# Gate rows formed inside the last projection block, and the gate tiles shared out anew between attention, sample and the loads for the last products

## The chip, the core and the metric

One NeuronCore of a Trainium2 chip runs the whole program. The metric is the time of one execution on the device in microseconds (us). TensorE (PE in the profile, with PEld for its weight loads) does the matmuls, VectorE (DVE), ScalarE (ACT) and GpSimd (POOL) the rest. Every transfer of this kernel is issued by the sync engine's queue (SP, SPq), which works through its list in order: an issue that waits for its data or its buffer holds up all issues behind it. Each engine likewise takes its own list in order.

## The reference

One layer of a hybrid decoder trunk for 1024 prompt rows and 32 sample rows (8 sequences of 4 new tokens). With fp32 inputs:

```
h = rmsnorm(x)
pool_in, pool_z, qk_pre, v, o_pre, m_z, if_pre, gate_pre = split(h @ w_in)
a  = (multiscale_pool(pool_in) * silu(pool_z)) @ w_pool_down
q, k = split(silu(causal_conv(qk_pre)))
i, f = split(if_pre + b_if)                 # 4 heads each: the gate rows
hc = mlstm_chunkwise(q, k, v, i, f, state)  # chunks of 128 rows, running C, n, m
bm = (head_rmsnorm(hc * sigmoid(o_pre)) * silu(m_z)) @ w_mlstm_down
g_a, g_b = split(sigmoid(gate_pre))         # 2 x 1024 columns: the gate tiles
x = x + (g_a * a + g_b * bm) @ w_out
x = x + (pe @ w_ple) * sigmoid(rmsnorm(x) @ w_ple_gate);  y = rmsnorm(x)
```

The sample rows use the same formulas with a state `C` of 512x512 per sequence and head (32 of them, 1 MB each), which is read, updated and written back.

## The kernel before

Every fp32 product is made from high and low parts: a tile is split into `whi` (ACT, line 286 or 288) and `wlo` (DVE, line 292 or 294), and `mm3` (lines 299 to 301) issues three matmuls for each 128 rows of the contraction. `load_w` (line 320) brings 256 columns of a weight in two halves through two buffers `wraw`.

The stages stand one behind the other in `run`:

1. `norm_in` and 20 projection blocks (q, k, v, o, z for each of 4 heads; `half_product`, line 603), which write q, k, v, o, z to DRAM. Near the end `plain_h` rebuilds the normalised input `hh`, `hl`.
2. `gates` forms the 8 gate rows i and f (48 matmuls of 352 columns, line 652), sends them through DRAM (`g8D`) and makes the decay tables of all chunks (`dt`, lines 767 and 790).
3. `merge_gates(range(8))`: 8 groups of 256 gate columns. A group is 6 chunks of 24 matmuls of 352 columns (three chunks are here called one gate tile: 128 columns for all 1056 rows; a group has two), each chunk evicted by a sigmoid (`sz`, line 1192) and each tile stored to DRAM (`sgD`, line 1194).
4. `attn`: 16 pairs of chunks (4 heads x 4). A pair loads `qk`, `v`, `o`, `zz` (lines 826 and 873; `v`, `o`, `zz` have one buffer each), makes two `num` products, updates `C` (the `kv` products) and transposes the result `o` (`attn_turn`, line 948). The buffer of `num` is single, so the second `num` of a pair waits until DVE has formed `o` from the first (line 936), which needs the loaded `o`.
5. `sample`: 32 steps; each loads a state `ct` (line 1051), multiplies it (`num`, line 1053), updates it (`kv`, line 1057; DVE line 1058) and stores it (line 1061), with three buffers. It ends with `hcS`, the sample rows of `hc`.
6. `pool_branch`: 4 groups, each 12 chunks of 24 matmuls against `hh`, `hl` and 6 short chunks against `poh`, `pol`.
7. `hc_tiles` loads the attention's result into `mvhA`, `mvlA` (buffers named `sz` again), then `downs` and two closing stages make the last products.

Stages overlap by a generator: `feed` sets work aside in the background, and each `fm` over the full contraction ends with `tick`, which takes `rate` further steps of it. Gates and attention are fed to the gate tiles, the sample to `pool_branch`. A scheduler then puts the instructions of all engines in a fixed order, so program order is a priority and not the final order.

Of the kernel before, what the change touches and what calls it, by code (L numbers as in the profile page):

```python
# [11 lines left out]
F32R = mybir.dt.float32r  # L12
AF = mybir.ActivationFunctionType
ALU = mybir.AluOpType
# [4 lines left out]
P = 128  # L19
# [4 lines left out]
NT = T + NS  # L24
H, DH = 4, 512
M = H * DH
KT = D // P
L = 128
NCH = T // L
CW = NT // 3  # L30
# [13 lines left out]
O_GB = O_GA + D  # L44


RATE_A, RATE_S = 10.0, 2.1
HT = T // 2


# [210 lines left out]
class Trunk:  # L261
# [369 lines left out]
                                      rhs=raw[k // 4][f][:, k % 4, :], start=k < 4, stop=k >= 4)  # L631
        return ps

    def gates(self):


        nc, I, O = self.nc, self.I, self.O
        a, d, c = self.ap_, self.dp, self.cp2
        raw = self.t(a, [P, KT, 8], "gw")
        nc.sync.dma_start(raw, I["w_in"][:, O_IF:O_IF + 8].rearrange("(k p) n -> p k n", p=P))  # L640
        wg = self.t(a, [P, KT, P], "gwh", F32R)
        nc.gpsimd.memset(wg.bitcast(F32), 0.0)
        self.hi(wg[:, :, 0:8], raw)
        self.lo(wg[:, :, 32:40], raw, wg[:, :, 0:8])
        g8 = self.t(a, [8, NT], "g8")
        g8l = self.t(a, [8, NT], "g8l")
        for j in range(3):
            s = slice(j * CW, (j + 1) * CW)
            ps = self.mmps()
            for k in range(KT):  # L650
                for x in range(2):
                    nc.tensor.matmul(ps[:, :CW], lhsT=wg[:, k], rhs=self.hmov[k][x][:, s], start=k == 0 and x == 0,
                                     stop=k == KT - 1 and x == 1)
            nc.scalar.activation(g8l[:, s], ps[32:40, :CW], AF.Copy)
            nc.vector.tensor_tensor(out=g8[:, s], in0=ps[0:8, :CW], in1=g8l[:, s], op=ALU.add)
        gD = self.t(d, [8, NT], "g8D")
        nc.sync.dma_start(gD, g8)
        yield True
        R, W = H * NCH, L + DS
        gi = self.t(a, [R, W], "gi")  # L660
        gf = self.t(a, [R, W], "gf")
# [31 lines left out]
        ps = self.miscps()  # L693
# [7 lines left out]
        for h in range(H):  # L701
# [11 lines left out]
                                op=ALU.subtract)  # L713
        nc.vector.tensor_tensor(out=half(rows[:, 2], 0), in0=half(rows[:, 2], 1), in1=half(en[:, 0], 0), op=ALU.add)
        ps = self.miscps()
# [12 lines left out]
        g = self.t(a, [R, W], "gg")  # L728
# [25 lines left out]
        ps = self.miscps()  # L754
# [8 lines left out]
        for h in range(H):  # L763
# [5 lines left out]
            for j in range(NCH // 2):  # L769
                for x in (0, 2):  # L770
                    nc.vector.scalar_tensor_tensor(out=dt[:, j, x], in0=dt[:, j, x], scalar=col(0, 2 * j + x // 2),
                                                   in1=self.cmask, op0=ALU.add, op1=ALU.add)
# [647 lines left out]
    def run(self):  # L1420
# [9 lines left out]
        d = self.dp  # L1430
# [29 lines left out]
        for n, _ in enumerate(blocks):  # L1460
            if n == 20 * 7 - 2 - 4:
                self.plain_h()
        _g.close()
        _w.close()
        _x.close()
# [8 lines left out]
        _m.close()  # L1474
        self.ap_, _a = self.pool("gates", "right")
        gates = self.gates()
        next(gates)
        self.pp, _p = self.pool("gates2")
        _s = []

        def rest():
            self.rate = 1.6
            yield from gates
            _a.close()
            self.atp, _at = self.pool("attn", "right")
            self.attn_setup()
            self.rate = RATE_A
            yield from self.attn()
            _at.close()
            self.sp, st = self.pool("sample", "right")  # L1490
            _s.append(st)
            self.rate = RATE_S
            yield from self.sample()
        self.feed(rest(), 1.6)
        self.merge_gates(range(8))
        while not _s:
            next(self.bg)
        _p.close()
# [2 lines left out]
        _p.close()  # L1501
        self.mpA, _ma = self.pool("movA")
        self.pp, _p = self.pool("gates3")
        first = self.hc_tiles(self.pp, 0, "A", "sz")
        self.drain()
        _s[0].close()
        _p.close()
# [39 lines left out]
```

## Time and profile before

| what | value |
|---|---|
| median of 3 runs | 2294.91 us (2289.3 to 2297.19) |
| the profiled execution | 2293.93 us, its span 2292.2 us |
| TensorE busy | 2191.0 us, 96% of the span |
| VectorE, ScalarE, GpSimd busy | 1247.5, 898.6, 139.9 us |
| mean granted TensorE clock | 0.976 of 2.4 GHz |
| the chain that ended last | PE 89%, DMA 6%, DVE 2% |
| moved to and from HBM | 310 MB, 135 GB/s over the span |

The table is read against TensorE: the rest of the span, some 101 us, is time in which it ran no matmul, and at a granted clock of 0.5 (1.2 GHz) its work takes twice as long.

### The profile page before, as it was taken

The page shows a single profiled execution, that of the slowest core. Times are in us where ns is not written, and L with a number is a line of the kernel's source. Part 1 is how long each engine was busy: PE and PEld are TensorE (multiplying, and loading weights), DVE is VectorE, ACT ScalarE, POOL GpSimd, SP SyncE. Part 2 cuts the span into 40 slices and gives each one's busy share as a digit, 9 for nine tenths or more (in the row PEclk, how much of TensorE's full clock was granted, in tenths as well). Part 3 has the DMA queues.
Part 4 walks back from the last instruction along what each step waited for, and adds up shares of the span by engine and source line. Part 5 has one row for each costly group of instructions (what it writes and reads, how often), then busy time and mean ns, then how long its engine had stood idle before and what let it go on. Part 6 is the DMA issues. An engine that isn't in the chain of part 4 may idle for free.

```text
span 2292.2 us, 37165 instructions
## 1 busy us (share of the span) xinstructions
PE 2191.0 (96%) x15071; PEld 1993.7 (87%) x15071; DVE 1247.5 (54%) x2063; ACT 898.6 (39%) x1634; POOL 139.9 (6%) x319
## 2 busy tenths in 40 slices
PE   5999999999999999899999999999994999999998
PEld 4789888989898989899999998877772999999998
DVE  7846465646644665336565665655664334443545
ACT  5535444534454454444333343322231431223443
POOL 2101010001100110000000000000000000000000
PEclk7999999999999999999999999999995999999999
DMA  4333332333232331384656454667766524323112
GB/s 140 98 99 104 98 106 74 112 101 108 74 120 88 100 103 53 107 282 135 202 169 198 152 168 161 204 246 271 262 217 217 166 94 131 104 75 132 52 47 81
DMA packets 235836, 312.52 MB, mean 136 GB/s; under 512 B 13722, under 2 KB 168946, under 8 KB 235664
## 3 DMA queue, kind: packets, MB, share of 16 engines
q1 hardware_dynamic: 235664, 310.15, 41.5%
q8 instruction: 118, 1.93, 0.3%
q14 instruction: 54, 0.44, 0.1%
HBM read 200.01 MB, written 110.45 MB: 135 GB/s over the span
## 4 chain that ended last, share of the span: by engine, by line
PE 89%; DMA 6%; DVE 2%; ACT 1%; issue 1%; SPq 0%; POOL 0%; DVEq 0%; POOLq 0%; ACTq 0%
PE mm L603 35%; PE mm L299 12%; PE mm L301 12%; PE mm L300 12%; PE misc L630 2%; PE num L1053 2%; PE misc L838 2%; DMA ct<-state_mlstm_C 2%; PE num L299 2%; PE num L300 1%; PE num L301 1%; PE kv L299 1%; DMA new_C_sample<-ct 1%; PE kv L300 1%; PE kv L301 1%; PE kv L1057 1%
## 5 line engine op out<-in xcount | busy, mean ns | idle before, releaser
L292 DVE TENSOR_TENSOR wlo<-wraw,whi 128x1024 fp32r<-128x1024 f32 (+1 forms) x196 | 235.2, 1200 | 275.9 <-ACT whi L286 273.5
L286 ACT ACTIVATE whi<-wraw 128x1024 fp32r<-128x1024 f32 (+1 forms) x196 | 203.6, 1039 | 241.9 <-PE mm L603 94.6
L299 PE MATMUL mm<-hh,whi 128*128 128x352 f32 x768 | 252.1, 328 | 6.3 <-ACT sz L1192 5.3
L301 PE MATMUL mm<-hh,wlo 128*128 128x352 f32 x768 | 251.8, 328 | 0.0
L300 PE MATMUL mm<-hl,whi 128*128 128x352 f32 x768 | 250.8, 327 | 0.0
L603 PE MATMUL mm<-whi,hl 128*128 128x256 f32 x768 | 217.6, 284 | 0.0
L603 PE MATMUL mm<-wlo,hh 128*128 128x256 f32 x768 | 214.8, 280 | 0.0
L603 PE MATMUL mm<-whi,hh 128*128 128x256 f32 x768 | 214.7, 281 | 0.0
L299 PEld LDWEIGHTS mm<-hh,whi 128*128 128x128 f32 x768 | 145.7, 190 | 12.2 <-ACT sz L1192 5.6
L242 DVE SCALAR_TENSOR_TENSOR z<-z,vcols,z 128x512 f32<-128x512 f32 (+1 forms) x192 | 143.9, 774 | 21.7 <-ACT z L240 14.6
L301 PEld LDWEIGHTS mm<-hh,wlo 128*128 128x128 f32 x768 | 145.8, 190 | 10.1 <-issue 9.2
L300 PEld LDWEIGHTS mm<-hl,whi 128*128 128x128 f32 x768 | 146.2, 190 | 7.5 <-issue 6.7
L603 PEld LDWEIGHTS mm<-whi,hh 128*128 128x128 f32 x768 | 145.0, 189 | 5.7 <-ACT part L256 3.3
L1058 DVE SCALAR_TENSOR_TENSOR ct<-ct,dec,kv 128x512 f32<-128x512 f32 x128 | 92.2, 742 | 98.1 <-PE kv L1057 75.7
L603 PEld LDWEIGHTS mm<-wlo,hh 128*128 128x128 f32 x768 | 144.5, 188 | 0.4
L603 PEld LDWEIGHTS mm<-whi,hl 128*128 128x128 f32 x768 | 144.4, 188 | 0.4
L97 ACT ACTIVATE s<-mm 128x512 f32<-128x512 f32 x120 | 71.4, 595 | 147.4 <-PE mm L603 146.0
L301 PE MATMUL mm<-mvhB,wlo 128*128 128x352 f32 x384 | 123.0, 321 | 0.8 <-DVE wlo L294 0.8
L300 PE MATMUL mm<-mvlB,whi 128*128 128x352 f32 x384 | 122.8, 321 | 0.0
L299 PE MATMUL mm<-mvhB,whi 128*128 128x352 f32 x384 | 119.7, 323 | 0.0
L603 PE MATMUL mm<-hh,whi 128*128 128x512 f32 x256 | 102.7, 402 | 1.4 <-DVE n4l L498 1.3
L603 PE MATMUL mm<-hl,whi 128*128 128x512 f32 x256 | 102.4, 400 | 1.3 <-DVE hl L292 1.3
(435 smaller groups left out, 5794.9 us busy)
## 6 DMA issues: line engine op xcount, KB each, us to landing
wraw<-w_in SPq DMA_DIRECT2D x112, 512.0 KB
ct<-state_mlstm_C SPq DMA_DIRECT2D x32, 1024.0 KB
new_C_sample<-ct SPq DMA_DIRECT2D x32, 1024.0 KB
qkD<-z SPq DMA_DIRECT2D x64, 256.0 KB
qk<-qkD SPq DMA_DIRECT2D x16, 1024.0 KB
sgD<-sz SPq DMA_DIRECT2D x16, 528.0 KB
sg<-sgD SPq DMA_DIRECT2D x16, 528.0 KB
vD<-z SPq DMA_DIRECT2D x32, 256.0 KB
```

What stands on the lines that cost most here:

```text
L97: tr.nc.scalar.activation(s, x, AF.Copy)
L242: nc.vector.scalar_tensor_tensor(out=acc[:, :tot], in0=z[:, o:o + tot], scalar=wc(o), in1=acc[:, :tot], op0=ALU.mult, op1=ALU.add)
L286: self.nc.scalar.activation(out, in_, AF.Copy)
L292: self.nc.vector.tensor_tensor(out=out, in0=in_, in1=hi.bitcast(F32), op=ALU.subtract)
L299: mm(ps, lhsT=sh, rhs=mh, start=start, stop=False)
L300: mm(ps, lhsT=sh, rhs=ml, start=False, stop=False)
L301: mm(ps, lhsT=sl, rhs=mh, start=False, stop=stop)
L603: mm(out, lhsT=st[k], rhs=mv[k], start=start and opens and k == 0 and n == 0, stop=stop and k == 3 and n == 2, skip_group_check=True)
L630: self.nc.tensor.matmul(ps[g, f * 256:(f + 1) * 256], lhsT=self.hs[:, k, :], rhs=raw[k // 4][f][:, k % 4, :], start=k < 4, stop=k >= 4)
L838: nc.tensor.matmul(out, lhsT=qk[:, 4 + d, i * L:(i + 1) * L], rhs=qk[:, d, i * L:], start=d == 0, stop=d == 3)
L1053: nc.tensor.matmul(num[32 * d:32 * d + 32, 0, :], lhsT=qm[:, b * P + d * NS:b * P + (d + 1) * NS], rhs=ct[:, d, :], start=b == 0, stop=b = ...
L1058: nc.vector.scalar_tensor_tensor(out=ct[:, d, :], in0=ct[:, d, :], scalar=self.dec[:, h * DB + b, 1:2], in1=kv, op0=ALU.mult, op1=ALU.add)
```

## The change

The gate rows move from the start of `gates` into a function `gate_rows`, called with `plain_h` inside the last projection block; they borrow its buffers (`z`, `whi`) and are stored in three parts. `attn` is taken at 16 steps for a gate tile, not 10, the sample at 1.85, not 2.1. Six groups of gate columns stay beside gates and attention; group 6 now stands behind `pool_branch`, and group 7 behind the loads of `hc_tiles`.

```diff
--- before.py
+++ after.py
@@ -44,7 +44,7 @@
 O_GB = O_GA + D
 
 
-RATE_A, RATE_S = 10.0, 2.1
+RATE_A, RATE_S = 16.0, 1.85
 HT = T // 2
 
 
@@ -631,19 +631,16 @@
                                       rhs=raw[k // 4][f][:, k % 4, :], start=k < 4, stop=k >= 4)
         return ps
 
-    def gates(self):
-
-
-        nc, I, O = self.nc, self.I, self.O
-        a, d, c = self.ap_, self.dp, self.cp2
-        raw = self.t(a, [P, KT, 8], "gw")
+    def gate_rows(self):
+
+        nc, I, g = self.nc, self.I, self.gp
+        raw = self.t(g, [P, 3 + HT + 56], "z", bufs=self.nz)[:, :KT * 8].rearrange("p (k n) -> p k n", k=KT)
         nc.sync.dma_start(raw, I["w_in"][:, O_IF:O_IF + 8].rearrange("(k p) n -> p k n", p=P))
-        wg = self.t(a, [P, KT, P], "gwh", F32R)
+        wg = self.t(self.wp, [P, KT, P], "whi", F32R, bufs=3)
         nc.gpsimd.memset(wg.bitcast(F32), 0.0)
         self.hi(wg[:, :, 0:8], raw)
         self.lo(wg[:, :, 32:40], raw, wg[:, :, 0:8])
-        g8 = self.t(a, [8, NT], "g8")
-        g8l = self.t(a, [8, NT], "g8l")
+        self.g8D = self.t(self.dp, [8, NT], "g8D")
         for j in range(3):
             s = slice(j * CW, (j + 1) * CW)
             ps = self.mmps()
@@ -651,11 +648,17 @@
                 for x in range(2):
                     nc.tensor.matmul(ps[:, :CW], lhsT=wg[:, k], rhs=self.hmov[k][x][:, s], start=k == 0 and x == 0,
                                      stop=k == KT - 1 and x == 1)
-            nc.scalar.activation(g8l[:, s], ps[32:40, :CW], AF.Copy)
-            nc.vector.tensor_tensor(out=g8[:, s], in0=ps[0:8, :CW], in1=g8l[:, s], op=ALU.add)
-        gD = self.t(d, [8, NT], "g8D")
-        nc.sync.dma_start(gD, g8)
-        yield True
+            g8 = self.t(g, [P, 3 + HT + 56], "z", bufs=self.nz)[:8, :CW]
+            nc.scalar.activation(g8, ps[32:40, :CW], AF.Copy)
+            nc.vector.tensor_tensor(out=g8, in0=ps[0:8, :CW], in1=g8, op=ALU.add)
+            nc.sync.dma_start(self.g8D[:, s], g8)
+
+    def gates(self):
+
+
+        nc, I, O = self.nc, self.I, self.O
+        a, d, c = self.ap_, self.dp, self.cp2
+        gD = self.g8D
         R, W = H * NCH, L + DS
         gi = self.t(a, [R, W], "gi")
         gf = self.t(a, [R, W], "gf")
@@ -1460,6 +1463,7 @@
         for n, _ in enumerate(blocks):
             if n == 20 * 7 - 2 - 4:
                 self.plain_h()
+                self.gate_rows()
         _g.close()
         _w.close()
         _x.close()
@@ -1474,7 +1478,6 @@
         _m.close()
         self.ap_, _a = self.pool("gates", "right")
         gates = self.gates()
-        next(gates)
         self.pp, _p = self.pool("gates2")
         _s = []
 
@@ -1492,7 +1495,7 @@
             self.rate = RATE_S
             yield from self.sample()
         self.feed(rest(), 1.6)
-        self.merge_gates(range(8))
+        self.merge_gates(range(6))
         while not _s:
             next(self.bg)
         _p.close()
@@ -1501,7 +1504,9 @@
         _p.close()
         self.mpA, _ma = self.pool("movA")
         self.pp, _p = self.pool("gates3")
+        self.merge_gates(range(6, 7))
         first = self.hc_tiles(self.pp, 0, "A", "sz")
+        self.merge_gates(range(7, 8))
         self.drain()
         _s[0].close()
         _p.close()
```

The scheduler's order shows the change at three places. Buffer numbers are part of the names.

First the sync queue around the end of the last block. `z` are the block's results, `zD` their place in DRAM, `wraw` the weights of the first gate columns, `gw` the raw weights of the gate rows. Before:

```order
L177 DMA zD_16_75<-z_8825 128x2x256
L177 DMA zD_16_75<-z_8878 128x2x256
L320 DMA wraw_8998<-w_in 128x4x256
L320 DMA wraw_9004<-w_in 128x4x256
L177 DMA zD_16_75<-z_8882 128x2x256
L640 DMA gw_8928<-w_in 128x8x8
L668 DMA bif_9091<-b_if 32x1x1 x2
```

and now:

```order
L177 DMA zD_16_75<-z_8841 128x2x256
L177 DMA zD_16_75<-z_8948 128x2x256
L320 DMA wraw_9001<-w_in 128x4x256
L320 DMA wraw_9007<-w_in 128x4x256
L177 DMA zD_16_75<-z_8952 128x2x256
L669 DMA gi_9092<-g8D_8717 32x1x128
L670 DMA gi_9092<-g8D_8717 32x1x4
```

The two `wraw` loads stand behind the last but one store of the block in both; the gate rows' weights are gone from here (they are loaded earlier), and reading the rows back (`gi`) now follows the block's last store at once.

Second, TensorE at a change of pairs in the attention, from the last transposes of one pair's `o` towards the second `num` of the next pair. In the kernel before, at the change from the tenth to the eleventh pair:

```order
L948 MATMUL misc_12442<-ident_112,o_12216 128x128 x4
L300 MATMUL num_12548<-Cl_9637,qh_12370 128x256
L301 MATMUL num_12548<-Ch_9636,ql_12371 128x256
L894 MATMUL misc_12594<-ident_112,qk_12355 128x128 x4
L299 MATMUL mm_12931<-hh_135,whi_12459 128x352
L300 MATMUL mm_12931<-hl_136,whi_12459 128x352
L301 MATMUL mm_12931<-hh_135,wlo_12460 128x352
```

and at the same change now:

```order
L951 MATMUL misc_12273<-ident_112,o_11967 128x128 x4
L897 MATMUL misc_12333<-ident_112,qk_12186 128x128 x4
L897 MATMUL misc_12394<-ident_112,qk_12186 128x128 x4
L299 MATMUL kv_12403<-vhi_1233_9628,kh_1698_12338 128x258
L300 MATMUL kv_12403<-vlo_1235_9630,kh_1698_12338 128x258
L299 MATMUL kv_12411<-vhi_1233_9628,kh_1698_12338 128x256
L300 MATMUL kv_12411<-vlo_1235_9630,kh_1698_12338 128x256
L301 MATMUL kv_12403<-vhi_1233_9628,kl_1699_12339 128x258
L299 MATMUL kv_12403<-vhi_1234_9629,kh_1707_12399 128x258
L300 MATMUL kv_12403<-vlo_1236_9631,kh_1707_12399 128x258
L301 MATMUL kv_12411<-vhi_1233_9628,kl_1699_12339 128x256
L299 MATMUL kv_12411<-vhi_1234_9629,kh_1707_12399 128x256
```

Before, 23 gate matmuls (`mm<-hh`, `mm<-hl`) stand among the 65 from these transposes to that second `num`; now it is 28 matmuls in all and none of them a gate's. Of the attention's `num` and `kv` matmuls (1632) 347 stood behind the last gate tile before, and 816 do now: heads 2 and 3 run without gate tiles beside them. Short changes of pair, with under 50 matmuls from the transposes to the second `num`, were two before, the last two with 39 and 37; now there are seven, with 32, 28, 45, 35, 45, 45 and 37, which is 267 together.

Third, TensorE at the end of the sample. Before, its last steps and the last transposes ran straight into the last products (`mm<-mvhA`):

```order
L1057 MATMUL kv_16743<-vst_16200,km_16732 128x512
L1053 MATMUL num_14232<-ct_16734,qm_14233 32x512 x4
L1065 MATMUL num_14232<-voz_16885,sel_120 32x512
L1057 MATMUL kv_16746<-vst_16200,km_16732 128x512
L1057 MATMUL kv_16749<-vst_16200,km_16732 128x512
L1071 MATMUL num_14232<-voz_16888,pb_14149 128x512
L1080 MATMUL misc_16904<-ident_112,shc_16895 128x128 x4
L1174 MATMUL misc_16969<-ident_112,np_2004_14285 47x128 x4
L1174 MATMUL misc_16985<-ident_112,np_2004_14285 47x128 x4
L299 MATMUL mm_17141<-mvhA_17010,whi_17119 128x352
```

Now they lie between the gate tiles of groups 6 and 7:

```order
L300 MATMUL mm_16784<-hl_136,whi_16605 128x352
L301 MATMUL mm_16784<-hh_135,wlo_16606 128x352
L1068 MATMUL num_13891<-voz_16810,sel_120 32x512
L1074 MATMUL num_13891<-voz_16813,pb_13808 128x512
L299 MATMUL mm_16876<-hh_135,whi_16865 128x352
L300 MATMUL mm_16876<-hl_136,whi_16865 128x352
L301 MATMUL mm_16876<-hh_135,wlo_16866 128x352
```

and the last products follow the last gate chunk:

```order
L299 MATMUL mm_17008<-hh_135,whi_16871 128x352
L300 MATMUL mm_17008<-hl_136,whi_16871 128x352
L301 MATMUL mm_17008<-hh_135,wlo_16872 128x352
L299 MATMUL mm_17144<-mvhA_16841,whi_17122 128x352
L300 MATMUL mm_17144<-mvlA_16842,whi_17122 128x352
L301 MATMUL mm_17144<-mvhA_16841,wlo_17123 128x352
```

On VectorE and ScalarE the splits of `mvhA` and `mvlA` moved ahead of the sigmoids of group 7: the first sigmoid of group 7 stands behind the last of the four splits.

## Rows read from the trace of the kernel before

**Rows 1.** Stretches: length, busy time by engine (x instructions), granted clock, DMA share, GB/s.

```profile
922.00:1000.00 78.00, 65.24 (x387) 64.00 (x386) 30.50 (x101) 39.09 (x51) 3.38 (x6) 0.91 0.58 169
1000.00:1360.00 360.00, 359.89 (x2634) 356.00 (x2633) 204.73 (x390) 137.66 (x274) 15.29 (x26) 1.00 0.58 185
1360.00:1420.00 60.00, 54.63 (x436) 52.44 (x435) 40.48 (x90) 23.25 (x48) 4.91 (x9) 0.96 0.35 111
1420.00:1710.00 290.00, 279.19 (x1603) 224.09 (x1603) 164.44 (x301) 75.91 (x138) 13.11 (x37) 0.98 0.69 240
1710.00:1775.00 65.00, 33.23 (x115) 17.39 (x114) 31.44 (x63) 13.03 (x30) 0.89 (x3) 0.65 0.66 232
```

**Rows 2.** The chain that ended last, 905 to 945 us: start, length, what.

```profile
908.76 1.22 DVE hl L292 x2
...
910.71 11.38 PE mm L603 x94
922.09 5.14 DMA wraw<-w_in
927.25 1.07 ACT whi L286
...
929.85 9.87 PE mm L652 x48
939.88 0.16 PE mm L300
```

**Rows 3.** TensorE's waits, 920 to 1000 us: in total, times, longest.

```profile
PE mm L652 <- DVE gwh L292: 7.4, 1, 7.4
PE mm L299 <- ACT sz L1192: 5.3, 1, 5.3
```

**Rows 4.** TensorE's instructions at the last two changes of pair, idle time before in brackets.

```profile
1377.61 0.55 PE L948 MATMUL misc<-ident,o 128*128 128x128 f32 x3 [0.29 <-DVE o L941]
...
1386.92 0.36 PE L299 MATMUL num<-Ch,qh 128*128 128x258 f32 x1 [2.12 <-DVE o L936]
...
1399.38 0.66 PE L948 MATMUL misc<-ident,o 128*128 128x128 f32 x4
...
1405.61 0.36 PE L299 MATMUL num<-Ch,qh 128*128 128x258 f32 x1 [0.69 <-DVE o L936]
```

**Rows 5.** The sync queue's issues of loads at these two changes of pair.

```profile
1376.92 0.37 SPq L873 DMA_DIRECT2D v<-vD  x1
1377.58 0.37 SPq L873 DMA_DIRECT2D zz<-zD  x1
1378.30 0.36 SPq L873 DMA_DIRECT2D o<-oD  x1
...
1400.07 0.36 SPq L873 DMA_DIRECT2D o<-oD  x1
```

**Rows 6.** The chain that ended last, 1355 to 1420 us.

```profile
1378.30 7.63 DMA o<-oD
```

**Rows 7.** TensorE's waits: first 1420 to 1710 us, then 1710 to 1775.

```profile
PE num L1053 <- DMA ct<-state_mlstm_C: 8.0, 3, 3.5
...
PE mm L299 <- ACT mvhA L286: 12.3, 1, 12.3
PE num L1053 <- DMA ct<-state_mlstm_C: 10.9, 3, 6.8
```

**Rows 8.** Stretches as in group 1, where the granted clock was halved.

```profile
1388.00:1391.40 3.40, 3.40 (x19) 3.40 (x18) 2.14 (x4) 0.73 (x2) 0.55 (x1) 0.51 0.00 0
...
1719.20:1732.90 13.70, 9.87 (x31) 6.30 (x30) 8.10 (x16) 1.74 (x3) 0.00 (x0) 0.50 0.63 195
1743.10:1780.60 37.50, 15.93 (x47) 9.89 (x48) 8.49 (x18) 5.79 (x13) 0.55 (x1) 0.50 0.52 181
```

**Rows 9.** The chain that ended last, 1690 to 1800 us.

```profile
1730.76 8.15 DMA new_C_sample<-ct
1738.92 9.21 DMA ct<-state_mlstm_C
```

## The prediction, made before the change was run

> **What bounds the kernel now.** I began with the page: TensorE is busy for 96% of the span, so a change can win what the other 101 us hold and what a halved clock costs, and no more. Then I cut the span into stretches [rows 1]. From 1000 to 1360 us, where the attention runs beside gate tiles, TensorE does not stop. It stops for 12.8 us (78 less 65.24) at the start of the gates, for 5.4 us in the 60 us of attention behind the last gate tile, for 10.8 us in the first 290 us of the pool branch, where the sample runs beside it, and for 31.8 us in the 65 us from there to the last products. In the first of these and in the last the granted clock is 0.91 and 0.65. For each stretch I then asked for TensorE's waits, and for the chain that ended last where a wait needed a cause.
>
> At the gates the wait of 7.4 us is for the split of the gate rows' weights, that of 5.3 us for a sigmoid [rows 3]. The chain [rows 2] shows the first: the last block's matmuls end at 922.09, a weight load lands 5.14 us later, ScalarE splits it (1.07), then the gate rows' own split can run, and their 48 matmuls take 9.87 us. Only at 939.88 does the first gate tile start.
>
> In the bare attention the second `num` of a pair waits for DVE's `o` [rows 4]. At the first such change 2.12 us are lost, and the cause is a load of `o` that takes 7.63 us [rows 6] with `v` and `zz` issued up to 1.4 us before it [rows 5].
>
> In the pool branch TensorE waits 8.0 us in 3 waits for states `ct`; from 1710 on 10.9 us for the last states and 12.3 us for the first split of the last products' input [rows 7]. A state's buffer is stored (8.15 us) and loaded again (9.21 us) before the step three later can run [rows 9]. With no other work left in TensorE's list at that point, this is bare waiting.
>
> **The sum, part by part.** It is made against the profiled execution, 2293.9 us (span 2292.2 and 1.7 around it). That lies 1 us under the median, which I add at the end.
>
> *Gate rows.* Now 17.8 us pass from the last block's end (922.09) to the first gate tile (939.88) [rows 2]. The 48 matmuls stay. They have 352 columns as a gate tile's, which start 0.16 us apart at full clock [rows 2], so 7.7 us of them now stand in the block. But the first gate tile's weights still wait behind the block's last but one store, so their load and split remain bare: 5.14 and 1.07 for the second half; the first half comes a little sooner, and I take 4.5 us (bounds 3.5 to 6.2). 12.2 us replace 17.8, a gain of 5.6. What hides the wait of the new matmuls for `plain_h`: its splits in the chain (`hl`, to 909.98) are done before the block's last 94 matmuls start at 910.71 [rows 2], and most of the new ones stand among or behind these. If that cover failed, each us late would be a us lost. The 5.3 us wait for the sigmoid comes from the decay tables' load, whose chain starts about one chunk sooner against TensorE; but ScalarE now puts two table changes of the gates ahead of the first sigmoid. I give it back 0.5 (0 to 5.3). This part: **-6 us** (-3 to -11).
>
> *Attention at 16 steps for a gate tile.* Nothing of it becomes longer in itself, but 816 of its matmuls run bare, not 347. Where does the stall go: to the load of `o`. From the last transposes to the second `num` TensorE had 6.64 us of work at the first bare change (1378.16 to 1384.80) and 4.88 us at the second (1400.04 to 1404.92), for 39 and 37 matmuls [rows 4], so about 0.15 us each; the seven changes now have 267 matmuls, 40 us. The time from the transposes to the second `num` was 8.76 us at the first and 5.57 at the second, where `v` was not in flight with the others [rows 4, 5]. These are the bounds. At 5.57 for all seven next to no wait is left (two, at the shortest); at 8.76 it is 61.3 less 40, or 21 us, of which 2.8 are there today. In the new order `v` is sometimes next to the other two and sometimes earlier, so I take the middle, 7.2: 10.4 less 2.8, or +7.6. A wait of 2.12 us was followed by 3.4 us at half clock [rows 8], which costs 1.7; I count three more of these, +5, and +1 for the smaller waits of 4.5 more bare pairs. This part: **+14 us** (+1 to +29).
>
> *Pool branch, sample and the way into the last products.* The 12 chunks moved here are the same work as before (46 us, taken out of the attention), and are a cover, not a cost. Today's waits from 1420 to 1775 are 42.6 us [rows 1]. Of these the waits in three groups (10.8) stay, since in the order the steps of the sample stand as close in the short chunks as before, and the fourth group gets its like, as it still has steps: 14.4, and 17 for the one more step in it. The wait for the last two states goes: the order has four gate chunks, 15 us, more between a state's release and its use. The 12.3 us go, but something else is late next: the first sigmoid of group 7 stands on ScalarE behind the fourth split of `mvhA`, which waits for a load into a buffer that a stored gate tile must free. TensorE has two banks for these chunks, so the third chunk waits. 3.5 us (bounds 0 and one load, 7.6). The start of the last products costs 2 (0 to 12.3, today's), since their first four input tiles are split early; small waits 1.5. Together 24, a gain of 18.6. The half clock cost 4.9 and 8.0 us in the two long stretches (half of 9.87 and 15.93 busy) [rows 8]; three short ones of 1.7 take their place, a gain of 7.8. This part: **-26 us** (-13 to -36).
>
> -6, +14 and -26 make -18: 2276, and **2277 us** against the median.
>
> **The rivals.**
>
> *Loads land in time.* If no change of pair waits (5.57 us each), the attention costs +1, and the sum is -31: **2264**. For it: at the second bare change the load was not what was waited for. Against it: 7.63 us at the first. The Trainium skill, DMA: Bandwidth & Descriptors, Anatomy of one DMA, fits a transfer (on GpSimd's path) as 2.0 us and bytes over 436 GB/s, so an estimate of 3.2 us for these 512 KB; by that rule no change would wait and this rival would hold. The row of 7.63 us with other loads in flight disagrees with it.
>
> *Every change waits in full.* At 8.76 us for all seven the attention costs 21 less 2.8, six more half-clock stretches (10) and 1: +29, the sum is -3: **2292**, no change that can be told. For it: three of the seven have less work than the first one had. The Trainium skill, TensorE: Matmul & The Clock Gate, HAM oscillation, describes a loop in which each wait for a transfer leaves the clock halved for the next tile, so that it is paid on every turn; by that rule all seven changes pay 1.7 us, as in this rival, where I count three more. The row at 1388 us agrees for one of them.
>
> *Slower.* The same place decides the other sign: if the way from the transposes to the second `num` takes over 10.1 us, the attention gives up more than the other parts win. At 10.5, 73.5 less 40 and 2.8, with 11 for the clock: +42, the sum +10, **2305**. For it: transfers of a head's `C` to HBM fall into one of these changes, and the load rate is higher with pairs closer together. Against it: 8.76 with three loads at once was the longest seen bare.
>
> *The hole moves.* If the loads and splits for the last products hold ScalarE in the midst of group 7 as long as they hold TensorE today, the last part wins only 9, by the states and half the clock: -1, **2294**. For it: ScalarE's order. Against it: the loads now start one gate tile earlier.
>
> **Chances and range.** The forecast 0.45, loads in time 0.17, every change in full 0.17, slower 0.10, the moved hole 0.09, something else 0.02. A measurement of this kernel tells about 0.3%, 7 us, from no change. Faster than that (below 2288) are nearly all of the first two and a little of the others, 0.66; within it most of the third and the fourth sort, 0.22; slower 0.12. The forecast's own range is 2267 to 2288; for eight in ten I take 2256 to 2300, from beyond rival one to between no change and the slower case.
>
> **What would show it.** After: no wait for `gwh`, gate row matmuls in the block without a wait for `plain_h`, and 4 to 6 us bare before the first gate tile. TensorE's waits for `o` in the last two heads near 10 us in sum (2 or 21 by the rivals), with the clock at half behind the long ones. Pool branch: three to four waits for `ct` of 1 to 4 us, none for the last two states, no stretch like 1743 to 1780, some us at the third chunk of group 7, and last products that start within 3 us of the last gate chunk. Most of all the prediction is wrong if transfers in the bare heads take longer than 8.76 us, or ScalarE's list stalls in group 7.

## The result, and the profile after

The changed kernel took 2266.63 us (2265.5 to 2272.91), a ratio of 0.9889 to the kernel before, with a 95% interval of 0.9849 to 0.9929. Measured again in five rounds it was 0.9871 (0.9852 to 0.9891). It is faster by some 28 us; the forecast was 2277, in a range of its own of 2267 to 2288, which the time misses by a hair, and a wide one of 2256 to 2300.

I cut both executions at the same events: the attention's first product, the sample's first, the first of the last products. The first fence has the two stretches of the kernel before, the second has those of the changed kernel, with the gates ahead of them and the last products behind (columns as in [rows 1]).

```profile
1006.30:1416.30 410.00, 405.58 (x2989) 399.61 (x2988) 243.48 (x472) 158.22 (x318) 20.20 (x35) 1.00 0.54 172
1416.30:1774.40 358.10, 314.47 (x1752) 243.42 (x1752) 197.01 (x372) 91.09 (x170) 14.00 (x40) 0.92 0.69 238
```

```profile
921.90:998.50 76.60, 69.07 (x435) 66.48 (x435) 32.16 (x103) 43.56 (x57) 4.43 (x10) 0.98 0.72 232
998.50:1381.20 382.70, 369.27 (x2701) 359.24 (x2700) 235.69 (x466) 148.07 (x300) 22.68 (x35) 0.98 0.53 169
1381.20:1750.00 368.80, 349.02 (x2040) 288.03 (x2040) 207.64 (x379) 103.77 (x190) 14.90 (x40) 0.97 0.70 242
1750.00:2264.90 514.90, 505.48 (x3690) 495.48 (x3690) 230.80 (x467) 166.38 (x402) 16.07 (x26) 0.99 0.30 99
```

The attention starts 7.8 us sooner. It is 27.3 us shorter, but 46 us of gate chunks have left it: it lost 18.7. The tail (pool branch, sample, late gate tiles) is 10.7 us longer with these 46 us in it: it won 35.3. The last products take 514.9 us, not 517.8 (the span of 2292.2 less 1774.4). Together -27.3, the difference of the spans. Of the tail's gain 23.8 us are idle time (43.6 to 19.8); the other 11.5 are busy time, at a clock of 0.97 instead of 0.92.

**Gates** (against [rows 2, 3]). The first of two groups of the gate rows' products by line (busy and mean ns of one, then idle time before them), then TensorE's waits from 900 to 999 us:

```profile
L649 PE MATMUL mm<-hh,whi 128*128 128x352 f32 x24 | 7.6, 324 | 0.0
```

```profile
PE mm L299 <- ACT whi L286: 4.1, 1, 4.1
PE mm L299 <- ACT sz L1195: 3.4, 4, 1.8
```

No wait stands before the 48 products any more. Bare before the first gate tile are 4.1 us, for the split of its weights.

**Attention** (against [rows 4, 6]). TensorE's waits from 999 to 1381 us; on the timeline the two longest, with the last transposes of the pair ahead of the second; and the loads of `o` in the chain that ended last:

```profile
PE num L299 <- DVE o L939: 8.3, 5, 3.4
```

```profile
1228.33 0.56 PE L299 MATMUL num<-vhi,ph 128*128 128x258 f32 x1 [3.36 <-DVE o L939]
...
1305.04 0.63 PE L951 MATMUL misc<-ident,o 128*128 128x128 f32 x4 [0.23 <-DVE o L944]
...
1314.61 0.36 PE L299 MATMUL num<-vhi,ph 128*128 128x258 f32 x1 [2.12 <-DVE o L939]
```

```profile
1220.54 6.77 DMA o<-oD
1266.41 6.98 DMA o<-oD
1305.95 7.67 DMA o<-oD
```

Behind three of the waits the clock is halved (against [rows 8]); in the tail it is so for four short stretches, two of which are shown last:

```profile
1227.20:1234.00 6.80, 5.67 (x24) 5.56 (x25) 3.83 (x8) 1.62 (x5) 0.55 (x1) 0.50 0.50 157
1275.00:1278.40 3.40, 3.40 (x18) 3.40 (x17) 2.87 (x5) 0.04 (x1) 1.45 (x1) 0.50 0.12 40
1315.90:1322.70 6.80, 5.33 (x27) 5.07 (x26) 5.58 (x11) 2.37 (x4) 1.14 (x1) 0.50 0.30 101
...
1681.20:1688.00 6.80, 4.80 (x17) 2.49 (x17) 3.73 (x6) 1.16 (x2) 0.00 (x0) 0.50 0.75 274
1728.90:1735.80 6.90, 5.33 (x18) 5.33 (x19) 2.51 (x6) 1.87 (x5) 0.00 (x0) 0.51 0.08 32
```

**Tail** (against [rows 7]). TensorE's waits from 1381 to 1752 us, and below them ScalarE's timeline where the longer wait for `sz` arises:

```profile
PE num L1056 <- DMA ct<-state_mlstm_C: 7.6, 5, 2.7
PE mm L299 <- ACT sz L1195: 6.4, 2, 4.9
```

```profile
1718.43 0.18 ACT L1078 ACTIVATION_READ_ACCUMULATOR voz<-shc 128x1 f32 x1
1727.56 1.06 ACT L286 ACTIVATE mvhA<-sz 128x1024 fp32r<-128x1024 f32 x1 [8.94 <-DMA sz<-hcD]
1728.52 0.57 ACT L286 ACTIVATE mvhA<-hcS 128x32 fp32r<-128x32 f32 x4
1729.00 1.04 ACT L286 ACTIVATE mvhA<-sz 128x1024 fp32r<-128x1024 f32 x1
1729.95 0.82 ACT L1195 ACTIVATE sz<-mm 128x352 f32<-128x352 f32 x2
```

ScalarE stands 8.94 us for one load, and two finished chunks of group 7 wait behind it for their sigmoids; TensorE, out of banks, waits 4.86 us, until the split and the one behind it are done and the first sigmoid has run.

### The profile page after: what moved, and what is told of

It reads as the page before. It is cut to its first block, busy times and chain, and to the rows that moved or that the text cites. A ratio compares the mean times of both kernels' runs of the same rounds, so it can differ in the third digit from the quotient of the medians.

```text
span 2264.9 us, 37166 instructions
## 1 busy us (share of the span) xinstructions
PE 2186.8 (97%) x15071; PEld 1993.7 (88%) x15071; DVE 1247.0 (55%) x2063; ACT 899.9 (40%) x1635; POOL 145.7 (6%) x319
## 4 chain that ended last, share of the span: by engine, by line
PE 87%; DMA 6%; DVE 3%; ACT 2%; issue 1%; SPq 1%; POOL 0%; DVEq 0%; POOLq 0%; ACTq 0%
PE mm L603 35%; PE mm L299 12%; PE mm L301 11%; PE mm L300 11%; PE misc L630 2%; PE misc L841 2%; PE num L1056 2%; PE num L299 1%; PE num L300 1%; PE num L301 1%; DMA ct<-state_mlstm_C 1%; PE kv L299 1%; PE kv L300 1%; PE kv L301 1%; DMA new_C_sample<-ct 1%; PE kv L1060 1%
## 5 line engine op out<-in xcount | busy, mean ns | idle before, releaser
L299 PE MATMUL mm<-hh,whi 128*128 128x352 f32 x768 | 254.0, 331 | 13.4 <-ACT sz L1195 8.2
```

The lines of the kernel that those rows point to most:

```text
L299: mm(ps, lhsT=sh, rhs=mh, start=start, stop=False)
```

## The experiments

All in five rounds, each set on one chip with the kernel before beside it.

| run | ratio to before, 95% interval | median, us |
|---|---|---|
| gate rows alone | 0.9935 (0.9918 to 0.9952) | 2280.3 |
| sharing alone | 0.9912 (0.9895 to 0.9929) | 2276.5 |
| whole change | 0.9871 (0.9852 to 0.9891) | 2267.0 |
| whole, `o` in halves | 0.9857 (0.9841 to 0.9873) | 2262.1 |
| whole, no tile behind the loads | 0.9857 (0.9840 to 0.9875) | 2261.8 |
| both of these | 0.9833 (0.9819 to 0.9847) | 2257.5 |
| both, sample at 1.7 | 0.9834 (0.9821 to 0.9846) | 2255.8 |
| whole, attention at 10 | 0.9907 (0.9893 to 0.9921) | 2272.5 |
| whole, both tiles behind the loads | 0.9942 (0.9928 to 0.9955) | 2281.0 |
| whole, sample at 2.1 | 0.9972 (0.9962 to 0.9981) | 2289.4 |
| one group moved, rates 13 and 1.95 | 1.0001 (0.9993 to 1.0010) | 2294.3 |
| gate rows and rates, no chunk moved | 1.0230 (1.0209 to 1.0250) | 2349.1 |

Diffs are against the changed kernel, but for the second.

### Gate rows alone

```diff
-RATE_A, RATE_S = 16.0, 1.85
+RATE_A, RATE_S = 10.0, 2.1
-        self.merge_gates(range(6))
+        self.merge_gates(range(8))
-        self.merge_gates(range(6, 7))
-        self.merge_gates(range(7, 8))
```

> The kernel before with the gate rows formed inside the last projection block, and nothing else: eight groups of gate columns, rates 10 and 2.1. My theory is that the change is a sum of three parts which hardly touch each other, and that this one is worth the 7.8 us by which the attention's first matmul came sooner (1006.3 before, 998.48 with the whole change): about 2287 us, no wait for the gate rows' weights, some 4 us bare before the first gate tile, and the waits for o (2.8 us), for ct and for the last products' input (12.3 us) all still there. Rival: the later stages wait for transfers and not for TensorE, so that what is won at the gates is waited for again in the pool branch: 2293 or more, with the ct waits longer by as much.

It won more, some 14 us. The attention starts at 1000.4, 5.9 sooner, as meant, and the hole is still there (TensorE's waits from 900 to 1800 us):

```profile
PE num L1056 <- DMA ct<-state_mlstm_C: 12.7, 6, 3.7
PE mm L299 <- ACT mvhA L286: 12.5, 2, 12.0
```

The rest comes late: up to the 22nd state the sample runs 6 to 9 us ahead of the kernel before, at the last state 16.4 (1731.8 against 1748.2). TensorE's lists of the two kernels are alike from the gates' end to there (956 to 1656 us in the kernel before, buffer numbers aside), and then place the last ten steps otherwise. So an edit at the gates changed the order 700 us later. By what way the scheduler passed it on is not shown. The rival falls.

### Sharing alone

```diff
@@ before.py @@
-RATE_A, RATE_S = 10.0, 2.1
+RATE_A, RATE_S = 16.0, 1.85
-        self.merge_gates(range(8))
+        self.merge_gates(range(6))
+        self.merge_gates(range(6, 7))
         first = self.hc_tiles(self.pp, 0, "A", "sz")
+        self.merge_gates(range(7, 8))
```

> The whole change but for the gate rows, which stay at the start of the gates. By my theory of three separate parts: the wait of 7.4 us for the gate rows' weights is back, the rest as in the changed kernel, so 2266.6 and 7.8, about 2274 us; from the attention's first matmul to the end within 2 us of the changed kernel. Rival: the parts hang together, so that the new sharing needs the earlier gate rows: 2280 or more; or does as well without them: 2269 or less.

2276.5, as forecast within 3 us. From the attention's first product to the end it took 1270.0 us, the whole change 1266.4 (1265.8 in a second execution, below): 4 more, not 2.

### The whole once more

> The changed kernel once more, unaltered, so that its ratio stands beside the others of this set on one chip. The two halves run alone gave 0.9935 and 0.9912. If they add, the whole is 0.9847, about 2260 us; if they share a part of their gain (both let the last states' waits go), it is nearer to its first measurement, 0.9889: 2267 us.

It falls between: the product of the two halves is 0.9848, just outside this interval, but within the error of all three. That the halves share a part is likely and not settled. The second profile (stretches cut as above) differs most in the attention; its last products take 517.8 us, as in the kernel before:

```profile
999.50:1377.80 378.30, 365.10 (x2702) 354.52 (x2701) 235.60 (x466) 148.14 (x300) 22.73 (x35) 1.00 0.55 172
1377.80:1747.50 369.70, 350.01 (x2040) 288.34 (x2040) 207.53 (x379) 103.77 (x191) 14.43 (x40) 0.97 0.71 241
```

The attention's loss is 14.3 here, not 18.7: it stands idle as long (13.2 us), but its clock is granted in full.

### `o` in two halves

```diff
-            v, o, z = [self.t(a, [P, 2, 512], x) for x in ("v", "o", "zz")]
+            v, z = [self.t(a, [P, 2, 512], x) for x in ("v", "zz")]
+            o = [self.t(a, [P, 512], f"o{i}") for i in range(2)]
...
+            for i in range(2):
+                nc.sync.dma_start(o[i], both(self.oD)[:, i])
...
+                if d == 1:
+                    self.attn_turn(h, 2 * j, o[0])
...
+            self.attn_turn(h, 2 * j + 1, o[1])
```

> The changed kernel, with the attention's o in two tiles of one chunk each, loaded one by one, and the transposes of the first half moved ahead of the last four products of the update of C, so that the first half's buffer is free and its load issued earlier; same memory, same arithmetic. My theory: what the attention lost is the late load of o, so its waits (8.3 us in 5) fall to under 2, the stretches at half clock behind the two longest go with them, and the attention takes 10 to 14 us less: about 2254 us. Rival: another load of the pair (v, zz or qk), or the two more transfers on the queue, is late next in its place: 2262 or more, with waits at num or kv for v, or for qk. If these waits were not what the attention lost, no change.

The waits for the load of `o` are gone, and others stand in their place. TensorE's waits from 999 to 1374 us, and what the chain that ended last now holds there:

```profile
PE num L299 <- ACT qh L286: 2.3, 2, 1.2
PE misc L955 <- DVE o L948: 2.1, 3, 1.2
PE num L300 <- DVE Cl L292: 1.4, 2, 0.7
```

```profile
1261.23 6.06 DMA zz<-zD
1311.00 5.41 DMA zz<-zD
```

The idle time of the attention fell from 13.2 to 11.2, its length from 378.3 to 374.6. My theory that `o` alone was late falls: the rival, the pair's next load (`zz`, used at line 948), holds. The total is not told apart from the whole change.

### No tile behind the loads

```diff
-        self.merge_gates(range(6, 7))
+        self.merge_gates(range(6, 8))
         first = self.hc_tiles(self.pp, 0, "A", "sz")
-        self.merge_gates(range(7, 8))
```

> The changed kernel with both groups 6 and 7 ahead of the loads for the last products, so that no gate tile stands behind them. My theory: TensorE then has no work while these four inputs are loaded and split; the wait of 12.3 us of before comes back with some us at half clock, and the 4.9 us wait for the sigmoid of group 7 and the 1.6 us at the start of the last products go: 2271 to 2277 us. Rival: with the earlier end of the attention and of the sample the loads are issued in time anyway, and it is the four gate chunks between the states that did the work: 2262 to 2267, the last products starting within 3 us of the last gate chunk.

My theory falls, the rival holds: the hole does not come back. The tail is even 6.5 us shorter than in the second profile of the whole change (363.2), and the last products 6.7 longer (524.5). One of their inputs comes later (TensorE waits 2.6 us for `mvhA`), but 4.6 of the 6.7 are busy time:

```profile
1376.50:1739.70 363.20, 347.11 (x2041) 285.78 (x2041) 203.92 (x374) 100.92 (x186) 14.95 (x40) 0.98 0.71 243
1739.70:2264.20 524.50, 510.45 (x3690) 498.64 (x3690) 234.80 (x472) 169.54 (x407) 16.13 (x26) 0.99 0.30 99
```

### Both tiles behind the loads

```diff
-        self.merge_gates(range(6, 7))
         first = self.hc_tiles(self.pp, 0, "A", "sz")
-        self.merge_gates(range(7, 8))
+        self.merge_gates(range(6, 8))
```

> The changed kernel with both late groups behind the loads for the last products (the change has one behind, an earlier run none). My theory: where the loads stand does not matter as long as twelve chunks are near; the wait of ScalarE for a load then holds the first sigmoids of group 6 in place of group 7: 2263 to 2270. Rival: the closing steps of the sample then stand on ScalarE among these splits, as they do with the sample at 2.1, and both wait: 2280 or more, with waits for sz over 12 us.

Slower than the whole by 14 us, as the rival had it; but the waits for `sz` are 5.7 us, not 12, no more than in the whole. What grew are the waits for `ct` (11.1) and those at the closing steps of the sample, which stand bare. By line, TensorE's last transposes of the sample, the column behind the second bar being the wait:

```profile
L1083 PE MATMUL misc<-ident,shc 128*128 128x128 f32 x4 | 1.1, 428 | 3.3 <-DVE shc L1080 3.3
```

This wait of 3.3 us is in the kernel before and in five runs (gate rows alone, this one, sample at 2.1, one group, no chunk moved), all at 2280 us or above. In the whole change and the other six it is under 0.6.

### The sample at 2.1

```diff
-RATE_A, RATE_S = 16.0, 1.85
+RATE_A, RATE_S = 16.0, 2.1
```

> The changed kernel with the sample at 2.1 steps for a gate tile, as before, not 1.85. My forecast left the ct waits at 17 us, and they measured 7.6. Theory one: the lower rate did it, since the steps stand further apart; at 2.1 the ct waits grow to 12 to 17 us, and the time to 2271 to 2276. Theory two: the twelve chunks behind the pool branch did it, over which the same steps are spread at either rate; within 2 us of the changed kernel, ct waits of 6 to 10 us.

Neither number was far enough: 22 us slower. TensorE's waits in its tail, 1370 to 1769 us:

```profile
PE mm L299 <- ACT sz L1195: 12.9, 3, 6.0
PE num L1056 <- DMA ct<-state_mlstm_C: 12.3, 5, 3.8
...
PE misc L1083 <- DVE shc L1080: 3.3, 1, 3.3
```

The `ct` waits grew as theory one said, but by 3 to 5 us only. Those for `sz` grew more, by 6 to 8, and the cause is ScalarE's list: the first sigmoid of group 6 now stands behind the sample's closing steps and an eviction that waits 4.29 us for a store (`npst`, 1715.56), that of group 7 behind a split that waits 7.00 us for its load (1745.98).

### Both better edits together

The two diffs above, of `o` in halves and of no tile behind the loads.

> The two earlier edits together: o in two halves, and both late groups ahead of the loads for the last products. They touch different stretches, so if stretches add, it wins what both won against the changed kernel (0.9857 each): about 2257 us. Rival: each of the two was worth nothing beyond the spread of a measurement, and so are both: within 3 us of e5_whole.

2257.5 us, what adding them gives, and this kernel is told apart from the whole change, as neither edit alone is.

### The same at 1.7

```diff
-RATE_A, RATE_S = 16.0, 1.85
+RATE_A, RATE_S = 16.0, 1.7
```

> The better kernel of the earlier set (o in two halves, both late groups ahead of the loads; 2257.5) with the sample at 1.7 steps for a gate tile, not 1.85. Theory one: the ct waits go with the pace, so they fall below the 8 to 9 us of 1.85 by 3 to 6 us: 2251 to 2255. Theory two: the pace is not what sets them, but where single steps fall in the order; no gain, 2256 to 2262. If the sample then ends too late, its rows are missing at the last products: 2265 or more, with a wait for hcS.

The same ratio as at 1.85, and `ct` waits of 6.3 us against 7.0 there: no gain that can be told, as theory two had it. The tail in itself is 7 us shorter than at 1.85 (363.0 there), and the last products 2 us longer; of the rest of the difference between profile (a span of 2251.1) and median I know nothing.

```profile
1373.50:1729.30 355.80, 342.17 (x2040) 285.46 (x2040) 201.45 (x366) 101.73 (x184) 14.42 (x40) 0.98 0.72 247
```

### The attention at 10

```diff
-RATE_A, RATE_S = 16.0, 1.85
+RATE_A, RATE_S = 10.0, 1.85
```

> The changed kernel with the attention at 10 steps for a gate tile, as before, not 16; the groups are shared out as in the change. My forecast put the attention's loss down to the rate. But its order hardly depends on it: of 1632 num and kv products 870 stand apart from gate tiles at 10, 810 at 16. Theory one: with six groups beside it the attention loses the same at either rate, and the rate decides little: within 5 us of the changed kernel's 2267. Theory two: the rate is what sets the sample's steps in place; at 10 the sample starts later in the program's order and its end falls too late, the ct waits grow past 12 us: 2275 or more.

2272.5 us lies between the two forecasts. The attention is as long (381.8), so its rate does not set its loss: theory one there. But the tail is 376.1 us long, 6.4 more than in the second profile of the whole, with more waits for `ct` (11.9) and `sz` (7.3): the rate places the sample's steps. (The profile is that of the longest of the six executions, 2279.2 us.)

### One group moved

```diff
-RATE_A, RATE_S = 16.0, 1.85
+RATE_A, RATE_S = 13.0, 1.95
-        self.merge_gates(range(6))
+        self.merge_gates(range(7))
-        self.merge_gates(range(6, 7))
         first = self.hc_tiles(self.pp, 0, "A", "sz")
         self.merge_gates(range(7, 8))
```

> The changed kernel with seven groups beside gates and attention and one behind the pool branch (ahead of the loads for the last products), with rates to match, 13 and 1.95: half of the chunks moved. If cost and gain go with the number of chunks moved, the attention gets back half of its loss (19 us, so 9) and the tail gives up half of its gain (35 us, so 17): 2272 to 2278. Rival: the first six chunks bring most of the tail's gain, since they cover the end of the sample, and the second six only cost the attention: 2264 or less.

The edit is not what the expectation says: it takes out the group ahead of the loads and leaves the one late group behind them, as the diff shows. So neither number was tested. There is no gain at all. The attention's loss is 9.7 (396.7, less 410.0, and 23 us moved), half, as expected. But the tail won only 1.7 (379.4, less 358.1 and 23). The longest of its waits, on ScalarE's timeline:

```profile
1748.12 1.06 ACT L286 ACTIVATE mvhA<-sz 128x1024 fp32r<-128x1024 f32 x1 [8.34 <-DMA sz<-hcD]
...
1753.94 1.06 ACT L286 ACTIVATE mvhA<-sz 128x1024 fp32r<-128x1024 f32 x1 [2.97 <-DMA sz<-hcD]
...
1756.53 1.06 ACT L286 ACTIVATE mvhA<-sz 128x1024 fp32r<-128x1024 f32 x1 [1.41 <-DMA sz<-hcD]
1757.60 1.28 ACT L1195 ACT_TABLE_LOAD   x1
1758.89 0.82 ACT L1195 ACTIVATE sz<-mm 128x352 f32<-128x352 f32 x2
```

All four splits stand ahead of the first sigmoid of the late group, as the loads stand ahead of it in the program, and TensorE waits 14.0 us for it (1759.41). No run has one late group alone ahead of the loads.

### Gate rows and rates, no chunk moved

```diff
-        self.merge_gates(range(6))
+        self.merge_gates(range(8))
-        self.merge_gates(range(6, 7))
-        self.merge_gates(range(7, 8))
```

> The changed kernel with all eight groups beside gates and attention, as before, and none behind the pool branch: gate rows early and both new rates, no chunk moved. My theory: the moved chunks, not the rates, cost the attention its time and saved the tail's; so the attention takes 404 to 410 us again (from its first matmul to the sample's first), the bare wait for the last products' input (10 to 13 us) is back, and the time is that of the gate rows alone, 2278 to 2284. Rival: the rates did it, since they bring the sample's steps forward: 2270 or less, with the last states long loaded when the pool branch ends.

The attention is near what was expected (412.0), the time is not: 2349 us. From the gate rows alone (2280.3) this run differs in the two rates only. They bring the sample's 32 states together within 20 chunks, and the tail stands idle for 78.2 us at a clock of 0.82, 31.2 of them waiting for states (the stretch, then TensorE's waits in it):

```profile
1412.30:1829.00 416.70, 338.46 (x1752) 244.98 (x1752) 202.06 (x372) 91.93 (x170) 12.54 (x40) 0.82 0.60 205
```

```profile
PE num L1056 <- DMA ct<-state_mlstm_C: 31.2, 12, 5.6
```

So rates and moved chunks are not two parts: without the moved chunks the new rates cost 69 us. Which of the two rates does it is open.

## Why the prediction was right, and where it was not

**Gate rows** (-6): right in mechanism and size, 5.9 alone, 7.8 and 6.8 in two executions of the change; bare 4.1 us against 4.5. Not foreseen was that the edit re-places the sample's last steps: run alone, its tail is shorter by as much again (351.3 us for 358.1).

**Attention** (+14): +18.7 and +14.3 in two executions. The wait was named rightly, with 8.3 and 7.4 us for `o` against 10.4. In the forecast's own measure, the way from the last transposes to the second `num`, the seven changes took 5.6 to 8.9 us, 7.4 on average for its 7.2 (TensorE's own work in them is 42 us, for its 40); the longest (1305.67 to 1314.61, and 9.2 us in the second execution) lies a little above the bound of 8.76, and none came to the 10.1 of the slower rival. (By the forecast's own sums the attention would have used up what the other parts win near 9.2 on average, not at 10.1.) Idle time grew by 9.0 and 8.8 us, for the 8.6 of its two terms.

The rest is busy time, +9.7 and +5.5, and that the +5 for the clock comes near it is luck: in the second execution one stretch of 3.4 us was halved, not three. "Nothing of it becomes longer in itself" does not hold. In two runs the attention's clock was full throughout, in the gate rows alone and in the one with no tile behind the loads:

```profile
1000.40:1408.80 408.40, 404.11 (x2990) 398.15 (x2988) 242.29 (x470) 157.39 (x316) 20.29 (x35) 1.00 0.54 169
```

```profile
999.30:1376.50 377.20, 364.06 (x2702) 353.24 (x2702) 235.41 (x466) 148.02 (x300) 22.75 (x35) 1.00 0.55 173
```

404.1 less the 46 us of gate chunks is 358, and 364 is 6 more for the same products; why, no run shows. The step that failed is the heading: I put the loss on "16 steps for a gate tile", and it is as large at 10. It comes from the two groups taken away.

**Tail** (-26): -35.3 and -34.4. The forecast left 24 us idle; 19.8 and 19.7 are. The mis-sized term is "14.4, and 17": up to the last state's product (1707 us) TensorE stands idle for 13.4 us, and 7.6 of these (9.2 in the second execution) are waits for `ct`. They come, as before, in a group's short chunks or just behind them: 1.4, 3.1 and 3.5 us in the first three groups then (and 10.9 from the fourth on), none in the first now, and 1.9, 2.7 and 2.7 in the other three. So three groups pay much the same, as forecast, but the fourth comes in the first one's place and not on top of it, and the one more step adds nothing that can be seen. That is not a matter of how many chunks stand between the states: there are 44 from the first state to the last before and 48 now, but in the six runs with 46 or 47 these waits measure 7.0 to 12.3 us. The third chunk of group 7 cost 4.9 and 3.2 for my 3.5, the start of the last products 1.6 for 2, and busy time gave back 11.5 and 10.4, not the 7.8 that I had counted from three stretches.

**The rivals.** The time is that of "loads land in time" (2264), by another way: the loads were late, as forecast, and the tail won what the forecast had not given it. The estimate by the Trainium skill's page DMA: Bandwidth & Descriptors, Anatomy of one DMA, 3.2 us for such a load, does not agree with the 6.77 to 7.67 measured here. "Every change waits in full" falls with 8.3 us for its 21, and with a clock that was halved behind three of the seven changes in one execution and one in the other. "The hole moves" is real as a mechanism (4.9 us here, 14.0 with one group moved); I gave it 0.09 for this setting, and a neighbouring one, with all of the late work behind the loads, shows it in full. That the tile behind the loads closes the hole was still my expectation of the run without one; it is not so.

**What closed the hole**, then? The first and last start of the sample's `num` products, by tile, in the changed kernel, in the one with one group moved, and in the one with gate rows and rates alone:

```profile
L1056 PEld LDWEIGHTS num<-ct,qm x256: 106/109/150, 1391.6 to 1706.4; 128*32 128x32 f32 x128
```

```profile
L1056 PEld LDWEIGHTS num<-ct,qm x256: 106/109/157, 1407.9 to 1717.8; 128*32 128x32 f32 x128
```

```profile
L1056 PEld LDWEIGHTS num<-ct,qm x256: 106/125/156, 1422.7 to 1688.1; 128*32 128x32 f32 x128
```

315, 310 and 265 us. In all kernels but the last it is 305 to 328, with 44 to 54 gate and pool chunks between the states and TensorE busy for 92 to 97% of the time; with 20 chunks the same states come through faster, but TensorE waits 31.2 us for them. So it is mostly TensorE's own list that spaces the states, and the question is what is left of that list at their end. Before, TensorE's other work was used up with the last state; now 8 to 10 of the late chunks, 30 to 38 us, are left behind it (3 at 1.7, where the others stand between the states), and the states' end and the loads for the last products pass beside them. Chunks left over are not enough: in the three kernels that lose 14 to 27 of the 28 us again (both tiles behind, sample at 2.1, one group) 6 to 10 are left behind the last state too, but ScalarE waits for a load or a closing step ahead of the very first sigmoid of the late groups; in the whole change only group 7 stands behind such a load. How much of their loss that makes is open: TensorE's waits for `sz` are 5.7, 12.9 and 14.0 us in the three, against 6.4 and 4.8 in the whole, so that it explains the last two better than the first.

## What to carry to other kernels

Work that depends on nothing is worth most where a chain of transfers ends, but only with the queues of the other engines in order: look in ScalarE's list for what stands ahead of the first eviction. A rate or a share of such a schedule is not to be judged by itself: here the new rates without the moved groups lost 2.3% against the kernel before, and one moved group, behind the loads, gave nothing. And when a stall for one of several loads is removed, price the next one before counting the gain.

## What the runs showed that I had not expected

Much the same waits do not always halve the clock: with 8.3 us of them for `o` the attention's clock was 0.98 (three halved stretches), with 7.4 it was 1.00 (one), 4.4 us of length apart. And the load of a 1 MB state at the end of the sample took 5.18 us in one kernel (gate rows alone, at 1716.7) and 9.21 in another [rows 9], with steps of the sample placed otherwise around it; what of the difference is placement was not tried.
